# When the weight sums of a seven-product pair are made: with the pair's first piece instead of five pieces ahead

## Chip, cores and metric

The kernel runs on one core of a Trainium2 chip. The metric is the device time of one execution in microseconds (us); the time given for a kernel is the median of its runs. The tensor engine is called PE (its weight loads PEld), the vector engine DVE, the scalar engine ACT, GpSimd POOL, and the queue that issues the weight loads from memory SP.

## The reference, cut to what matters

Two decoder layers over 256 tokens of width 2048. Each layer is a token mixer followed by a gated feed-forward network with a causal convolution; all of it is products with large float32 weights.

```python
h = h + gla_mixer(...)      # ends in   o @ w_out      (2048 x 2048: "go" in the kernel)
h = h + conv_ffn(...)       # rms_norm(h) @ w_up, conv, silu(a)*u, @ w_down ("dn0")
k_blk, v_blk, k_mean = shared_kv(h, ...)
h = h + moba_mixer(...)     # ends in   o @ w_out      (2048 x 2048: "mo")
h = h + conv_ffn(...)       # "dn1"
```

The change touches the two output projections of the mixers, `go` and `mo`, and nothing else by its text.

## The kernel before

**Weights as a stream.** All weights pass through one `WeightStream`. A chunk is 128 x 2048 float32 (1 MB), loaded by SP (L96) into one of three buffers `wraw`. PE multiplies in a format of fewer bits, so each piece of up to 1024 columns of a chunk is split in two: ACT casts the high part (`whi`, L140), DVE subtracts it from the source and so makes the low part (`wlo`, L141). PE then does three products for each: high by high, low activation by high weight, high activation by low weight. A chunk's buffer is free for the next load when its last piece has been split. Most split pieces lie in three buffers each (`parts`); some pieces of the projections lie in a larger pool instead (`slot`).

**Pairs and seven products.** The output and down projections (`down`, L690 on) work through eight (or 22) pairs of 256 input rows, in two blocks of 1024 output columns. A block's order of pairs is written out in `ORDERS`; for the second block of `go` and for both of `mo` it is `0 2 1+ 3+ 4 | 5 6 7`. A plain pair needs two pieces of 1024 columns. A pair with a `+` takes seven products of quarters instead of eight, and needs sums of its weight quarters: its pieces are `b11` (the first 512 columns), `wide` (the second 1024), `t13` and `t24` (1024 each, sums). `_sums` makes `t13` and `t24` on DVE: L106 over 1024 columns, L107 and L108 over 512 columns each.

**When a piece is asked for.** `prefetch(i)` runs ahead of the product step `i`: the split of piece `n` is written down when `n` is within `AHEAD` (2) steps, plus 1 for pieces of projections, plus 2 for those in `deep`, which are the pieces of `go` and `mo`. Before the split of piece `n`, it looks through the next few pieces and, where one of them opens a seven-product pair, makes sure of that chunk's load and writes down its sums. In `go` and `mo` it looked at five pieces from `n` on.

**What sets the order.** The program is written down in one sequence; the framework's scheduler, with a timeline of its own, then sets each engine's order and the places of the buffers. Each engine works strictly through its own order, so an instruction that waits holds up what stands behind it.

**Ends of a block.** Products accumulate in PSUM (`acc`, three buffers of two banks, and two single banks `p`). At the last seven-product pair of a block ACT and DVE read the sums out into four tiles `c` (L756 to L760), POOL adds the residual to them by DMA (L762, from `x_tok` in `go`). Then come the tail pairs: first for the left half of the columns (products 2 and 4), then for the right (3 and 8), and after each half DVE adds the accumulator into `c` (L771). Products 2 and 3 share one accumulator `acc`, so the first right-half product of the tail waits until L771 has read the left half. PE transposes the finished columns (L795) while the next block runs; ACT (L253) and DVE (L255) make the next layer's operand `xw` from them, and the up-projection (L290, L293) follows.

Of the kernel before, what the change touches and what calls it, by code (L numbers as in the profile page):

```python
# [57 lines left out]
class WeightStream:  # L58
# [59 lines left out]
    def prefetch(self, i):  # L118
        nc = self.nc
        while self.n_split < len(self.halves):  # L120
            n = self.n_split
            c, o, kind = self.halves[n]
            if n > i + self.AHEAD + (kind != "plain") + 2 * (n in self.deep):
                break
            self._dma(c + 1)
            for c_, _, kind_ in self.halves[n:n + (5 if n in self.deep else 3)]:
                if kind_ == "b11" and c_ not in self.sums:
                    self._dma(c_ + 1)
                    self._sums(c_)
            src = self.sums[c][kind] if kind in ("t13", "t24") else self.tiles[c][:, o:o + 1024]  # L130
            if kind == "b11":
                src = src[:, :512]
            if kind != "plain" and n % 4 == 3 or n in self.deep and n % 2:
                hi, lo = self.slot([128, 1024], F32R, "whi"), self.slot([128, 1024], F32R, "wlo")
            else:
                hi = self.parts.tile([128, 1024], F32R, name="whi")
                lo = self.parts.tile([128, 1024], F32R, name="wlo")
            for a, b in ((0, 512), (512, 1024)) if n < 2 else ((0, src.shape[1]),):
                with self.tc.issue_after(self.first) if n + a else nullcontext():
                    one = nc.scalar.copy(hi[:, a:b], src[:, a:b])  # L140
                two = nc.vector.tensor_sub(lo[:, a:b], src[:, a:b], hi[:, a:b].bitcast(F32))  # L141
            self.latest = [one.ins, two.ins]
            self.split[n] = (hi, lo)
            self.n_split += 1
            if kind == "t24":
                del self.sums[c]
            if kind == "wide" and o == 1024 or kind == "plain" and (
                    self.n_split == len(self.halves) or self.halves[self.n_split][0] != c):
                del self.tiles[c]
                self._dma(c + 4)  # L150
# [969 lines left out]
```

## Time and profile before

| | |
|---|---|
| median of 3 runs | 2187.78 us (2187.05 to 2189.07) |
| profiled execution | 2188.65 us, its span from first to last instruction 2186.9 us |
| PE busy | 2169.1 us, 99% of the span |
| DVE busy | 1598.8 us, 73% |
| ACT busy | 1285.1 us, 59% |
| granted TensorE clock, mean | 0.999 |
| `go` on PE | 292 to 384 us of the span |
| `mo` on PE | from before 1385 to 1470 us |

Times in the rows are us from the span's start. A timeline row is: start, duration, engine, line, operation, tiles (out<-in), shape, count, and in brackets the idle time before it with what ended it. A row of the chain of waits is: start, duration, engine, tile and line. A row of the stretches is: the stretch, its length, then per engine busy us with the number of instructions, the granted clock, the share of the DMA engines that were busy, and GB/s. One product of 128 x 512 is shown with 0.39 us but the next begins 0.227 us after it, since products are pipelined.

### The profile page before, as it was taken

To read this page: it belongs to the slowest core of one execution; us is meant where nothing else is said; L and a number is where in the kernel's file an instruction comes from. 1 tells how busy PE (TensorE), PEld (TensorE's weight loads), DVE (VectorE), ACT (ScalarE), POOL (GpSimd) and SP (SyncE) were. 2 spreads that over 40 slices of the span, in tenths; PEclk is the share of its full clock that TensorE was granted. 3 is DMA by queue.
4 is the path that set the end of the run, shared out by engine and by line. 5 is a ranking of instruction groups with operands and counts; after the bars stand their busy time and mean duration, and the time that the engine had idled before them with its cause. 6 is when DMAs were issued, how large, how long until landed. Compare 5 with 4: busy or idle time off the path is not lost.

```text
span 2186.9 us, 26959 instructions
## 1 busy us (share of the span) xinstructions
PE 2169.1 (99%) x9693; PEld 1793.5 (82%) x9693; DVE 1598.8 (73%) x2202; ACT 1285.1 (59%) x1858; POOL 301.5 (14%) x448
## 2 busy tenths in 40 slices
PE   9999999999999999999999999999999999999999
PEld 7888887888888888887888888888888888887887
DVE  6655587667776767978967787776777676769887
ACT  6555765556555556555556676555656565655554
POOL 1011111111111111010013242011111111110000
PEclk9999999999999999999999999999999999999999
DMA  8465577577777777575677787676677777785655
GB/s 315 179 231 209 184 243 257 203 249 234 249 236 245 241 240 240 203 248 195 232 248 264 276 272 233 203 238 229 233 248 237 246 239 247 235 242 201 229 202 173
DMA packets 92248, 510.11 MB, mean 233 GB/s; under 512 B 13729, under 2 KB 14769, under 8 KB 42194
## 3 DMA queue, kind: packets, MB, share of 16 engines
q1 hardware_dynamic: 60722, 417.53, 54.1%
q0 software_dynamic: 30816, 90.28, 15.3%
q8 instruction: 76, 1.25, 0.2%
q10 hardware_dynamic: 576, 0.58, 0.1%
q14 instruction: 58, 0.48, 0.1%
HBM read 463.22 MB, written 45.11 MB: 232 GB/s over the span
## 4 chain that ended last, share of the span: by engine, by line
PE 91%; DMA 4%; DVE 3%; issue 1%; ACT 1%; SPq 0%; DVEq 0%; ACTq 0%
PE acc L290 44%; PE acc L293 22%; PE acc L730 13%; PE p L730 9%; DMA wraw<-w_dn 2%; DVE wlo L141 1%; DMA wraw<-w_go 1%; ACT whi L140 1%; DMA w2s<-w2a 0%; PE sT L561 0%; PE o L578 0%; DMA wraw<-w_v 0%; DVE t L106 0%; PE acc L795 0%; PE s L912 0%
## 5 line engine op out<-in xcount | busy, mean ns | idle before, releaser
L141 DVE TENSOR_TENSOR wlo<-wraw,whi 128x1024 fp32r<-128x1024 f32 (+1 forms) x786 | 929.9, 1190 | 446.4 <-ACT whi L140 425.5
L140 ACT CAST whi<-wraw 128x1024 fp32r<-128x1024 f32 (+1 forms) x786 | 799.6, 1027 | 675.4 <-PE acc L290 444.2
L290 PE MATMUL acc<-whi,xw 128*128 128x512 f32 x3840 | 952.2, 390 | 2.7 <-ACT whi L140 2.3
L290 PEld LDWEIGHTS acc<-whi,xw 128*128 128x128 f32 x3840 | 719.7, 188 | 154.1 <-ACT whi L140 3.1
L293 PE MATMUL acc<-wlo,xw 128*128 128x512 f32 x1920 | 514.1, 389 | 0.0
L293 PEld LDWEIGHTS acc<-wlo,xw 128*128 128x128 f32 x1920 | 360.2, 188 | 74.8
L730 PE MATMUL p<-whi,hid 128*128 128x512 f32 x572 | 204.1, 390 | 0.0
L730 PE MATMUL acc<-whi,hid 128*128 128x512 f32 x506 | 169.4, 389 | 0.0
L140 ACT CAST whi<-t 128x1024 fp32r<-128x1024 f32 x82 | 85.4, 1051 | 87.5 <-DVE t L108 25.3
L667 POOL DMA_DIRECT2D upT<-turned x176 | 114.1, 655 | 144.8 <-DMA turned<-z 55.9
L290 PE MATMUL acc<-whi,xkv 128*128 128x512 f32 x512 | 128.8, 391 | 0.0
L661 POOL DMA_DIRECT2D turned<-z x44 | 34.1, 775 | 680.1 <-DVE z L657 617.5
L730 PEld LDWEIGHTS p<-whi,hid 128*128 128x128 f32 x572 | 107.4, 188 | 22.2
L730 PE MATMUL acc<-whi,comb 128*128 128x512 f32 x328 | 107.7, 394 | 4.6 <-ACT whi L140 4.5
L730 PEld LDWEIGHTS acc<-whi,hid 128*128 128x128 f32 x506 | 95.0, 188 | 19.7
L290 PEld LDWEIGHTS acc<-whi,xkv 128*128 128x128 f32 x512 | 94.6, 188 | 18.6
L730 PE MATMUL p<-wlo,hid 128*128 128x512 f32 x286 | 106.3, 390 | 2.6 <-DVE wlo L141 2.6
L141 DVE TENSOR_TENSOR wlo<-t,whi 128x1024 fp32r<-128x1024 f32 x82 | 98.6, 1218 | 7.6 <-ACT whi L140 5.3
L676 ACT ACTIVATE au<-upT,cs 128x256 f32<-128x256 f32 x176 | 96.0, 595 | 10.8 <-DMA upT<-turned 10.7
L730 PE MATMUL acc<-wlo,hid 128*128 128x512 f32 x253 | 92.3, 390 | 0.8 <-DVE wlo L141 0.8
L762 POOL DMA_DIRECT2D c<-rows x24 | 21.2, 1073 | 463.2 <-DVE c L757 451.7
L682 DVE SCALAR_TENSOR_TENSOR au<-upT,cs,au 128x254 f32<-128x254 f32 x176 | 80.1, 477 | 0.0
(251 smaller groups left out, 1952.8 us busy)
## 6 DMA issues: line engine op xcount, KB each, us to landing
wraw<-w_up SPq DMA_DIRECT2D x176, 1024.0 KB, 4.9
wraw<-w_dn SPq DMA_DIRECT2D x88, 1024.0 KB, 4.8
turned<-z POOLq DMA_DIRECT2D x44, 512.0 KB, 3.5
upT<-turned POOLq DMA_DIRECT2D x176, 128.0 KB, 4.7
wraw<-w_g SPq DMA_DIRECT2D x16, 1024.0 KB, 4.8
wraw<-w_go SPq DMA_DIRECT2D x16, 1024.0 KB, 6.3
wraw<-w_mq SPq DMA_DIRECT2D x16, 1024.0 KB, 5.8
wraw<-w_kk SPq DMA_DIRECT2D x16, 1024.0 KB, 6.0
```

The source lines that it names most:

```text
L140: one = nc.scalar.copy(hi[:, a:b], src[:, a:b])
L141: two = nc.vector.tensor_sub(lo[:, a:b], src[:, a:b], hi[:, a:b].bitcast(F32))
L290: T.matmul(ps[:, t, :], xs(kt)[:, x0 + 128 * t:x0 + 128 * t + 128], hi[:, c:c + 512], start=kt == 0 and x0 == 0, stop=False)
L293: T.matmul(ps[:, t, :], xs(kt)[:, 128 * t:128 * t + 128], lo[:, c:c + 512], start=False, stop=kt == KT - 1)
L661: nc.gpsimd.dma_start(turned[J].rearrange("(a i) r q c -> (i r) a (q c)", a=4), z.rearrange("p (a q) t c -> p a (q t c)", a=4))
L667: nc.gpsimd.dma_start(f[32 * q:32 * q + 32].rearrange("p a (i c) -> p (a i) c", i=4), turned[J][:, :, q, :].rearrange("a r c -> r a c"))
L676: A.activation(au[:, i, :], t[:, i, :], AF.Identity, bias=col(cb + n), scale=col(cw + 2 * 2 * FT + n))
L682: V.scalar_tensor_tensor(au[:, i, 2:], t[:, i, :S - 2], col(cw + n), au[:, i, 2:], op0=OP.mult, op1=OP.add)
L730: T.matmul(p[n], x[xi], w[wi][:, 512 * f:512 * f + 512], start=n not in begun, stop=left[n] == 0)
L762: nc.gpsimd.dma_start(r[n], res(n // 2, 2 * b + n % 2), accum_op=OP.add)
```

## The change

For the pieces of `go` and `mo`, `prefetch` looks at one piece instead of five: the sums of a seven-product pair are written down when its own first piece (`b11`) is split, two pieces ahead of the first use of `t13`, and no longer up to four pieces earlier.

```diff
-            for c_, _, kind_ in self.halves[n:n + (5 if n in self.deep else 3)]:
+            for c_, _, kind_ in self.halves[n:n + (1 if n in self.deep else 3)]:
                 if kind_ == "b11" and c_ not in self.sums:
                     self._dma(c_ + 1)
                     self._sums(c_)
```

The instructions are the same in number and kind. What the diff doesn't tell is that the scheduler sets other orders, and other buffers, around them. Three places matter below. Numbers behind names tell buffers apart; in the second block of `go` the chunk of pair 0 is `wraw_2567`, of pair 2 `wraw_2608`, of pair 1+ `wraw_2648`, and of pair 3+ `wraw_2687` before and `wraw_2682` now.

ACT, at the start of the second block of `go`, before (a `whi` from `wraw` of 512 columns is a `b11`, one from `t13` a sum):

```order
L140 CAST whi_2644<-wraw_2548 128x1024
L140 CAST whi_2709<-wraw_2608 128x1024
L317 ACTIVATE junk_2703,ss_n_2419<-c0_2585 128x512
L317 ACTIVATE junk_2707,ss_n_2419<-c2_2587 128x512
L140 CAST whi_2767<-wraw_2648 128x512
L140 CAST whi_2683<-wraw_2567 128x1024
```

and further on in the same order:

```order
L253 ACTIVATE xw_2748<-acc_2743,cs_85 128x256
L140 CAST whi_2844<-wraw_2687 128x512
L253 ACTIVATE xw_2757<-acc_2743,cs_85 128x256
L140 CAST whi_2870<-t13_2762 128x1024
L140 CAST whi_2783<-wraw_2648 128x1024
```

The same two stretches of ACT now:

```order
L140 CAST whi_2644<-wraw_2548 128x1024
L140 CAST whi_2678<-wraw_2567 128x1024
L140 CAST whi_2720<-wraw_2608 128x1024
L140 CAST whi_2704<-wraw_2608 128x1024
L317 ACTIVATE junk_2698,ss_n_2414<-c0_2585 128x512
```

```order
L140 CAST whi_2807<-t13_2757 128x1024
L140 CAST whi_2778<-wraw_2648 128x1024
L140 CAST whi_2844<-wraw_2682 128x512
L253 ACTIVATE xw_2752<-acc_2738,cs_85 128x256
L140 CAST whi_2823<-t24_2758 128x1024
L140 CAST whi_2870<-t13_2839 128x1024
```

The second half of pair 0's chunk has moved ahead of pair 2 and of the `b11` of pair 1+, and the `wide` piece of pair 1+ (`whi_2783`, now `whi_2778`) no longer stands behind the `b11` and `t13` of pair 3+.

DVE, at the turn from the first to the second block of `go`, before:

```order
L141 TENSOR_TENSOR wlo_2645<-wraw_2548,whi_2644 128x1024
L771 TENSOR_TENSOR c0_2585<-c0_2585,acc_2420 128x512
L771 TENSOR_TENSOR c2_2587<-c2_2587,p4_2421 128x512
L141 TENSOR_TENSOR wlo_2710<-wraw_2608,whi_2709 128x1024
L771 TENSOR_TENSOR c3_2588<-c3_2588,p8_2422 128x512
L106 TENSOR_TENSOR t13_2662<-wraw_2648 128x1024
L141 TENSOR_TENSOR wlo_2768<-wraw_2648,whi_2767 128x512
```

and now:

```order
L141 TENSOR_TENSOR wlo_2645<-wraw_2548,whi_2644 128x1024
L141 TENSOR_TENSOR wlo_2679<-wraw_2567,whi_2678 128x1024
L141 TENSOR_TENSOR wlo_2721<-wraw_2608,whi_2720 128x1024
L771 TENSOR_TENSOR c0_2585<-c0_2585,acc_2415 128x512
L771 TENSOR_TENSOR c2_2587<-c2_2587,p4_2416 128x512
L141 TENSOR_TENSOR wlo_2705<-wraw_2608,whi_2704 128x1024
```

The first read of the accumulator (L771 into `c0`) has moved behind the low parts of pair 0's second half and of pair 2's first half; the sums L106 have left this place.

PE, at the end of `go`, where the up-projection begins (`whi_3070`), before, with the engines that an instruction waits for:

```order
L730 MATMUL acc_2797<-wlo_2990,go_2625 128x512 x2
L290 MATMUL acc_3137<-whi_3070,xw_2748 128x512 [waits DVE_49,PE_49]
L290 MATMUL acc_3137<-whi_3070,xw_2748 128x512 x7
L293 MATMUL acc_3137<-wlo_3071,xw_2748 128x512 x4
L290 MATMUL acc_3137<-whi_3105,xw_2757 128x512 [waits Activation_49]
L290 MATMUL acc_3137<-whi_3105,xw_2757 128x512 x7
L293 MATMUL acc_3137<-wlo_3106,xw_2757 128x512 x4
L290 MATMUL acc_3137<-whi_3123,xw_3012 128x512 [waits Activation_49]
L795 MATMUL hf_3150<-mk_86,c1_2943 128x2x2x32 [waits DVE_49]
```

and now:

```order
L730 MATMUL acc_2792<-wlo_2990,go_2625 128x512 x2
L290 MATMUL acc_3137<-whi_3070,xw_2743 128x512 [waits DVE_49,Activation_49]
L290 MATMUL acc_3137<-whi_3070,xw_2743 128x512 x7
L293 MATMUL acc_3137<-wlo_3071,xw_2743 128x512 x4
L795 MATMUL hf_3150<-mk_86,c1_2943 128x2x2x32
```

The transposes of `c1` (written by the last L771 of the block) no longer wait for DVE, since the first product of the up-projection, which stands ahead of them, has waited for that L771 already: its accumulator is now the one that this L771 reads. `mo` has the same difference at its end.

## Rows read from the trace of the kernel before

**Rows 1.** Page, part 1: busy us, share, instructions of each engine.
```profile
PE 2169.1 (99%) x9693; PEld 1793.5 (82%) x9693; DVE 1598.8 (73%) x2202; ACT 1285.1 (59%) x1858; POOL 301.5 (14%) x448
```
**Rows 2.** Timeline of PE, second block of `go`.
```profile
346.45 0.62 PE L730 MATMUL p<-wlo,go 128*128 128x512 f32 x2
350.58 0.79 PE L730 MATMUL acc<-whi,comb 128*128 128x512 f32 x1 [3.51 <-ACT whi L140]
...
355.92 0.84 PE L730 MATMUL acc<-whi,comb 128*128 128x512 f32 x3
```
**Rows 3.** Stretch behind that wait: busy us by engine, clock, DMA share, GB/s.
```profile
350.58:354.10 3.52, 3.52 (x9) 2.80 (x10) 3.52 (x5) 3.52 (x5) 0.00 (x0) 0.52 0.21 28
```
**Rows 4.** Chain of waits, 323 to 376 us.
```profile
323.28 8.27 DMA wraw<-w_go
331.65 1.06 ACT whi L140
...
337.49 1.15 DVE wlo L141
338.65 7.27 DMA wraw<-w_go
...
347.37 1.14 DVE t L106
348.54 2.00 ACT whi L140 x2
...
375.17 2.04 PE p L730 x9
```
**Rows 5.** Timeline of DVE, turn of the blocks of `go`.
```profile
316.52 1.22 DVE L141 TENSOR_TENSOR wlo<-wraw,whi 128x1024 fp32r<-128x1024 f32 x1 [1.06 <-ACT whi L140]
317.66 0.68 DVE L757 TENSOR_TENSOR c<-c,acc 128x512 f32<-128x512 f32 x1
...
329.33 0.69 DVE L771 TENSOR_TENSOR c<-c,acc 128x512 f32<-128x512 f32 x1 [3.19 <-PE acc L730]
...
332.73 1.23 DVE L141 TENSOR_TENSOR wlo<-wraw,whi 128x1024 fp32r<-128x1024 f32 x1 [2.11 <-ACT whi L140]
```
**Rows 6.** Timeline of PE: first right-half product of the tail of block one.
```profile
330.27 1.08 PE L730 MATMUL acc<-whi,go 128*128 128x512 f32 x4
```
**Rows 7.** Loads of `w_go`, all 16: time from issue to landing.
```profile
DMA to landing us min/median/max: 4.7/6.3/8.3
```
**Rows 8.** Stretches while the residual is added by DMA, and just after.
```profile
320.00:327.00 7.00, 7.00 (x32) 5.78 (x32) 6.14 (x7) 4.62 (x7) 2.65 (x3) 1.00 0.77 120
327.00:332.00 5.00, 5.00 (x24) 4.13 (x23) 1.28 (x2) 0.35 (x1) 1.14 (x2) 1.00 1.03 375
```
**Rows 9.** Timeline of DVE: one part of `xw`, one half sum.
```profile
348.42 0.48 DVE L255 SCALAR_TENSOR_TENSOR xw<-acc,cs,xw 128x256 fp32r<-128x256 f32 x1
348.82 0.68 DVE L107 TENSOR_TENSOR t<-t,wraw 128x512 f32<-128x512 f32 x1
```
**Rows 10.** Timelines of PE and DVE where the up-projections begin.
```profile
384.37 2.00 PE L290 MATMUL acc<-whi,xw 128*128 128x512 f32 x8
384.95 0.68 DVE L771 TENSOR_TENSOR c<-c,acc 128x512 f32<-128x512 f32 x1
1470.17 2.00 PE L290 MATMUL acc<-whi,xw 128*128 128x512 f32 x8
1470.74 0.68 DVE L771 TENSOR_TENSOR c<-c,acc 128x512 f32<-128x512 f32 x1
```
**Rows 11.** Timelines of DVE and PE, turn of the blocks of `mo`.
```profile
1417.37 0.69 DVE L771 TENSOR_TENSOR c<-c,acc 128x512 f32<-128x512 f32 x1 [2.52 <-PE acc L730]
1420.38 1.23 DVE L106 TENSOR_TENSOR t<-wraw 128x1024 f32<-128x1024 f32 x1 [2.32 <-DMA wraw<-w_mo]
1421.52 1.22 DVE L141 TENSOR_TENSOR wlo<-wraw,whi 128x1024 fp32r<-128x1024 f32 x1
1421.48 1.07 PE L730 MATMUL acc<-whi,ox 128*128 128x512 f32 x4
```
**Rows 12.** Stretches with the longest PE waits outside `go`: start of the kernel, `mo`.
```profile
11.40:13.50 2.10, 0.15 (x1) 0.00 (x0) 0.56 (x2) 1.09 (x2) 0.00 (x0) 1.00 1.04 423
13.50:17.00 3.50, 3.48 (x15) 2.85 (x16) 2.89 (x4) 1.89 (x4) 0.00 (x0) 1.00 1.02 406
1390.00:1400.00 10.00, 9.40 (x49) 7.36 (x48) 8.77 (x12) 7.53 (x12) 0.00 (x0) 1.00 0.28 107
```

## The prediction

> **What bounds the kernel now.** I read the busy shares first, then the timeline of the tensor engine for its gaps, then the chain of waits behind each gap. The tensor engine is busy 99% of the span [rows 1], so only a place where it stands still, or runs at the lower clock, can give anything back; DVE and ACT matter where a product waits for them. In the two stages that the change touches there is one such place of size: in the second block of `go` PE ends a run of products that begins at 346.45 and starts the next at 350.58, after 3.51 us idle that an ACT cast ended [rows 2]. Behind it the granted clock is 0.52, half of the full 2.4 GHz, for 3.5 us [rows 3]. The whole loss: from the product at 346.45 to that at 355.92 are 9.47 us [rows 2] with 18 products in them. Nine undisturbed ones take 2.04 us [rows 4], 0.227 each, so 18 take 4.08. **The place costs 5.4 us**, some 3.7 of waiting and 1.7 of low clock.
>
> Who made PE wait is in the chain [rows 4]: a load issued at 338.65 lands 7.27 us later; then comes a sum (L106, to 348.51), then two ACT casts from 348.54 to 350.54, then the product. By the order before, the load is the chunk of pair 3+, and the two casts are the `t13` of pair 3+ and, behind it, the `wide` piece of pair 1+. PE needs the second. It could have been cast long before, but stood in ACT's order behind two pieces of a later pair. And that pair's load was issued late because its buffer came free only with the DVE subtraction at 337.49, the second half of pair 0, which stood behind the sums and the `b11` of pair 1+.
>
> In `mo` the PE loss between 1390 and 1400 is 0.6 us of idle [rows 12]; it is where the attention values are still being made, and the change moves nothing there that PE waits for. I leave it.
>
> **The change, part by part.** No instruction is added or removed, and the order of SP's loads is the same. All gain or cost lies in PE's waits.
>
> *The old wait.* Now ACT casts the second half of pair 0 right after its predecessors, so the buffer is free, and the load of pair 3+ issued, about 11 us earlier; and the `wide` piece of pair 1+ stands ahead of everything of pair 3+. Both causes of the wait are gone: **-5.4 us**. It can't give more, since nothing else there holds PE; if one cause stayed, some of it would.
>
> *The turn of the blocks of `go`.* Before, DVE read the left half of the accumulator (L771) at 329.33, as soon as PE had finished it, and was done at 330.02 [rows 5]; PE went on with the right half at 330.27 [rows 6] without a wait. Now this L771 stands behind the low part of pair 2's first half. That one needs the load that the chain shows at 323.28 with 8.27 us to its landing at 331.55, then an ACT cast [rows 4]; before, it ran at 332.73 [rows 5], where nobody waited for it. What is queued behind it now is L771, and PE behind that. Price: landing 331.55, hand-over and cast 1.15, subtraction 1.14, L771 0.69, hand-overs 0.1: 334.6 against 330.27, 4.3 us. Part of that moves: before, DVE began the read-out L757 behind a subtraction that had waited 1.06 us for a late load [rows 5]. With the sums gone from ACT and DVE that load comes earlier; the residual's DMAs, and the load behind them, follow about 1.0 us sooner. So **+3.3 us**. The bounds come from the landing time. The loads of `w_go` take 4.7 to 8.3 us, median 6.3 [rows 7]. Issued at 322.3, a median landing gives 328.6 + 3.05 = 331.65, a wait of 1.4; the shortest gives none. I take the long one because the reason for it stays: from 320 to 327 the DMA engines are 0.77 busy but move 120 GB/s, the residual's slow transfers, and only then 375 GB/s [rows 8]; this load is issued into them again. Ends: 0 and 4.3.
>
> Here the clock is a second cost. The 3.5 us wait before was followed by the half clock [rows 3]; a wait of 2.1 us at the kernel's start was not: the stretch after it has 1.00 [rows 12]. A wait of 3.3 lies between, nearer to the one that cost 1.7. The Trainium skill (TensorE: Matmul & The Clock Gate, HAM oscillation — how this bites in real kernels) says that waits for a load between groups of products throttle the array, so that each next group starts cold; by that rule the turn costs 3.3 + 1.7 and the sum below is 1.7 higher, by the row of the shorter wait it is as it stands. I count it as a rival.
>
> *The sums of pair 3+.* They are now made after those of pair 1+ and after its low parts, shortly before use. From the four transposes that end ahead of pair 1+, PE's new order has 38 products to the first that reads the `t13` of pair 3+: 38 x 0.227 = 8.6 us. In that time: one ACT part of `xw` (0.5), on DVE two parts of `xw` (0.40 from one start to the next), two half sums (0.6 to 0.7), a `b11` (0.6), three low parts (1.14 each) and L106 (1.2) [rows 4, 9], 7.3 together, then the cast (1.06) and hand-overs (0.3): 9.2. **+0.6 us**; ends 0 and 2.2, the last being one sum and one cast in full view.
>
> *The first product of the up-projection*, after `go` and after `mo`. Its accumulator is now the one that the block's last L771 reads. In the trace before, that product started at 384.37 while L771 ran from 384.95 to 385.63; had it waited, it would have started at 385.68, 1.3 us later. In `mo`: 1470.17 against 1471.42, 1.3 again [rows 10]. DVE's order there still has one subtraction ahead of L771. **+1.3 us twice**; ends 0.9 each (the L771 and its hand-overs alone, which can't be hidden as PE's own last product feeds it) and 1.8.
>
> *The turn of the blocks of `mo`* has the same new order as that of `go`. There L771 ended at 1418.06 and PE needed it at 1421.48, 3.4 us of slack; the low part that is now ahead of it ran at 1421.52, but behind an L106 that had waited 2.32 us for another load and is no longer ahead [rows 11]. Unmoved it would make PE wait 2.0 us, moved up by the 2.3 nothing: **+0.2**, ends 0 and 2.0.
>
> Sum: -5.4 + 3.3 + 0.6 + 1.3 + 1.3 + 0.2 = **+1.3 us** on the span of 2186.9. The profiled execution took 2188.65, its span and 1.75 around it; the median of the runs is 2187.78. I add the difference to the median: **2189.1 us**.
>
> **Rivals.** *The clock falls at the new wait* (slower). Place: the turn of the blocks of `go`. Price: 3.3 us of wait and then 1.7 of half clock, as behind the old wait: +3.0, 2190.8; with the full 4.3 it is +4.0, and with a second such wait in `mo` up to +5. It decides from a PE idle time somewhere between 2.1 and 3.5 us. For it: the new wait is close to the old one. Against: it is a little shorter, and when the clock falls need not be the same in every run.
>
> *The load of pair 2 lands sooner* (faster). At the median landing the turn costs 1.4: -0.6, 2187.2; at the shortest it costs nothing: -2.0, 2185.8. For it: the load is issued a little earlier against the residual's DMAs, and the other loads of `go` mostly land sooner. Against: those DMAs move up with it.
>
> *The change doesn't do what it says*: pair 3+ still lands late and the old wait stays beside the new ones: +6.7, 2194.5. For it: the same three load buffers. Against: the casts that free the buffer stand ahead now.
>
> *None of the new waits is seen*: -5.4, 2182.4. For it: nothing but that PE was never stopped at these places before. Against: three of them follow from the order and from times in the trace.
>
> **How the numbers follow.** A measurement of this kernel can tell about 0.2% from no change, 4.4 us: below 2183.4 is faster, above 2192.2 slower. The forecast 0.43 (its own range 2187.5 to 2190.3); clock falls 0.30, of which 0.05 above 2192.2; sooner landing 0.17; old wait stays 0.05; no new wait 0.05. So faster 0.05, within 0.85, slower 0.10. The range goes from 2185.5, below the end of the sooner landing, to 2192.3, the clock rival with its bounds; it leaves out the last two cases and that rival's tail.
>
> **What would show it.** In the profile after, PE runs through 340 to 360 us without a wait. Around 330 it waits about 3.3 us for a DVE L771 that stands behind a low part released by an ACT cast that a `w_go` load released. The stretch behind it shows the clock at 1.00 or near 0.5, which settles the first rival. A wait of 1.3 us stands before the first L290 of both up-projections. The prediction is wrong if the wait around 330 is under 1 us or over 5, if an ACT cast still stops PE near 350, or if time is lost outside `go` and `mo`, where the order is the same.

## The result and the profile after

The changed kernel takes 2202.5 us (median of six runs, 2197.0 to 2204.7) against 2189.3 for the kernel before on the same chip (six runs too, 2187.1 to 2196.0): **a ratio of 1.0053, 95% interval 1.004 to 1.0065, half a per cent slower**. The profiled execution took 2202.19 us, its span is 2200.4: 13.5 us more than the span of before. Predicted was +1.3.

PE has the same instructions as before [rows 1] and is busy 6 us longer, in part because more of them run at half clock:

```profile
PE 2175.3 (99%) x9693; PEld 1795.7 (82%) x9693; DVE 1598.8 (73%) x2202; ACT 1282.4 (58%) x1858; POOL 301.8 (14%) x448
```

The list of PE's waits over the whole span (columns: who waited for whom, us in total, how often, longest) has three lines that end in DVE's L771, the add that reads a finished accumulator into the residual's tile. The list of before has no such line.

```profile
PE acc L795 <- DVE c L771: 3.9, 2, 2.3
...
PE acc L730 <- DVE c L771: 3.1, 1, 3.1
PE acc L290 <- DVE c L771: 2.6, 1, 2.6
```

Where the 13.5 us arise is read by comparing the start of the same product in both traces. The first right-half product at the turn of `go` goes from 330.27 [rows 6] to 333.81, +3.5. Past the place of the old wait PE is level again (+0.2 near 381). The first product of the up-projection goes from 384.37 [rows 10] to 389.54, and behind the half clock there PE is 6.9 late. The first down-projection adds 1.2. The turn of `mo` adds 4.0, after 0.3 gained ahead of it, and the first product behind `mo` goes from 1470.17 [rows 10] to 1482.92, 12.75 late. So, read where the lag is steady and rounded one by one: **up to the old wait +0.2, end of `go` +6.7, first down-projection +1.2, `mo` up to its turn -0.3, turn of `mo` +4.0, end of `mo` +1.1, the rest +0.7.**

*The turn of `go`* went as forecast but for the clock: DVE's timeline shows the low part that waited for ACT's cast, L771 behind it, and PE's timeline the wait for L771.

```profile
331.94 1.23 DVE L141 TENSOR_TENSOR wlo<-wraw,whi 128x1024 fp32r<-128x1024 f32 x1 [5.43 <-ACT whi L140]
333.08 0.68 DVE L771 TENSOR_TENSOR c<-c,acc 128x512 f32<-128x512 f32 x1
```
```profile
333.81 1.20 PE L730 MATMUL acc<-whi,go 128*128 128x512 f32 x4 [3.07 <-DVE c L771]
```

The clock then fell to half for a part of the stretch. The stretch behind that wait (columns: window, length, PE busy and products, granted clock, DMA share, GB/s), and those behind the two other large waits:

```profile
334.00:339.00 5.00, 5.00 (x16) 0.66 0.89 265
...
389.00:393.00 4.00, 3.46 (x9) 0.60 0.26 99
...
1435.00:1438.00 3.00, 3.00 (x10) 0.55 0.51 191
```

*The end of `go`* is where the forecast missed most. DVE's L771 there waits for no product: it waits for the residual's DMA, 5.59 us for one tile and 1.67 for the next, and a low part and half an `xw` stand between that one and the last L771. PE waits at the transposes of line 795 and again at the first L290.

```profile
384.23 0.69 DVE L771 TENSOR_TENSOR c<-c,p 128x512 f32<-128x512 f32 x1 [5.59 <-DMA c<-x_tok]
386.58 0.69 DVE L771 TENSOR_TENSOR c<-c,p 128x512 f32<-128x512 f32 x1 [1.67 <-DMA c<-x_tok]
387.19 1.22 DVE L141 TENSOR_TENSOR wlo<-wraw,whi 128x1024 fp32r<-128x1024 f32 x1
388.32 0.48 DVE L255 SCALAR_TENSOR_TENSOR xw<-acc,cs,xw 128x256 fp32r<-128x256 f32 x1
388.72 0.68 DVE L771 TENSOR_TENSOR c<-c,acc 128x512 f32<-128x512 f32 x1
```
```profile
384.97 0.55 PE L795 MATMUL acc<-mk,c 128*128 128x128 f32 x3 [1.55 <-DVE c L771]
...
389.54 2.66 PE L290 MATMUL acc<-whi,xw 128*128 128x512 f32 x6 [2.63 <-DVE c L771]
```

*The turn of `mo`* is the same thing, with 5.98 and 2.55 us of waiting in DVE; it is the first of the two that PE waits for:

```profile
1433.88 0.69 DVE L771 TENSOR_TENSOR c<-c,p 128x512 f32<-128x512 f32 x1 [5.98 <-DMA c<-rows]
1437.12 0.69 DVE L771 TENSOR_TENSOR c<-c,p 128x512 f32<-128x512 f32 x1 [2.55 <-DMA c<-rows]
```
```profile
1434.63 0.90 PE L795 MATMUL acc<-mk,c 128*128 128x128 f32 x3 [2.34 <-DVE c L771]
```

The kernel before was already near this. There the same L771 of `go` and of `mo` start at

```profile
377.18 0.69 DVE L771 TENSOR_TENSOR c<-c,p 128x512 f32<-128x512 f32 x1
...
1422.88 0.69 DVE L771 TENSOR_TENSOR c<-c,p 128x512 f32<-128x512 f32 x1
```

and the trace has their tiles' residual landing at 377.16 and 1422.85: each had waited some 0.15 us for it. So a landing that is later, against DVE's own order, holds DVE up at once; the prediction did not look at it.

Why is the residual late? The view of line 762, which issues it, second block of `go`, of before and then of after: the four transfers were issued 4.8 us (the first) to 2.0 us (the last) later, and the longest took 14.4 us instead of 8.3.

```profile
L762 POOL DMA_DIRECT2D c<-x_tok x4: 880/912/1287, 364.5 to 370.1; - x4
...
DMA to landing us min/median/max: 6.6/7.3/8.3
```
```profile
L762 POOL DMA_DIRECT2D c<-x_tok x4: 882/914/1291, 369.3 to 372.1; - x4
...
DMA to landing us min/median/max: 8.2/11.2/14.4
```

The DMA view of the second half of these transfers says what they met. Of before (372.0 to 378.5), and of after (378 to 385); columns: queue, packets, MB, share of 16 engines; q0 carries POOL's transfers, q1 the weight loads.

```profile
q0 software_dynamic: 508, 1.04, 80.8%
q1 hardware_dynamic: 72, 0.46, 23.9%
```
```profile
q1 hardware_dynamic: 256, 1.97, 69.4%
q0 software_dynamic: 255, 0.47, 36.1%
```

Before, the residual had the engines nearly alone, since no load was issued between 367.9 and 377.1. After, two loads of `w_up` go out at 374.2 and 377.5, and both queues send the same number of packets, 36 per us: the residual's carry 2 KB, the weights' 8 KB, so it gets a fifth of the bytes. The Trainium skill (DMA: Bandwidth & Descriptors, Queues, rings and completion order) says that a DMA engine takes turns between the queues it has work for, a whole packet from one before it switches, and by its count a packet is typically a group of some 9 to 17 descriptors. 256 against 255 of the profile's packets agree with turns of equal size; how large a turn is, these rows do not show.

The first four loads of `w_up` in SP's timeline, of before and of after:

```profile
361.41 15.98 SPq L96 DMA_DIRECT2D wraw<-w_up  x4
```
```profile
365.77 12.07 SPq L96 DMA_DIRECT2D wraw<-w_up  x4
```

### The profile page after: what moved, and what is told of

It is laid out like the page before. It is cut to its first block, busy times and chain, and to the rows that moved or that the text cites. A ratio compares the mean times of both kernels' runs of the same rounds, so it can differ in the third digit from the quotient of the medians.

```text
span 2200.4 us, 26957 instructions
## 1 busy us (share of the span) xinstructions
PE 2175.3 (99%) x9693; PEld 1795.7 (82%) x9693; DVE 1598.8 (73%) x2202; ACT 1282.4 (58%) x1858; POOL 301.8 (14%) x448
## 3 DMA queue, kind: packets, MB, share of 16 engines
q0 software_dynamic: 30816, 90.28, 15.3%
q8 instruction: 76, 1.25, 0.2%
## 4 chain that ended last, share of the span: by engine, by line
PE 82%; issue 8%; DMA 5%; DVE 3%; POOL 1%; ACT 1%; SPq 0%; DVEq 0%; POOLq 0%; ACTq 0%
PE acc L290 42%; PE acc L293 21%; PE acc L730 10%; PE p L730 7%; DMA wraw<-w_dn 2%; DVE wlo L141 2%; DMA c<-x_tok 1%; DMA c<-rows 1%; DMA w2s<-w2a 0%; POOL turned L393 0%; DMA probs<-z 0%; PE sT L561 0%; PE o L578 0%; ACT whi L140 0%; DMA wraw<-w_v 0%
## 5 line engine op out<-in xcount | busy, mean ns | idle before, releaser
L290 PE MATMUL acc<-whi,xw 128*128 128x512 f32 x3840 | 954.2, 390 | 5.6 <-DVE c L771 2.6
L290 PEld LDWEIGHTS acc<-whi,xw 128*128 128x128 f32 x3840 | 720.7, 188 | 158.2 <-ACT xw L253 5.4
L730 PE MATMUL p<-whi,hid 128*128 128x512 f32 x572 | 204.1, 390 | 0.0
L730 PE MATMUL acc<-whi,hid 128*128 128x512 f32 x506 | 169.4, 389 | 0.0
L290 PE MATMUL acc<-whi,xkv 128*128 128x512 f32 x512 | 128.8, 391 | 0.0
L730 PEld LDWEIGHTS p<-whi,hid 128*128 128x128 f32 x572 | 107.4, 188 | 22.3
L730 PEld LDWEIGHTS acc<-whi,hid 128*128 128x128 f32 x506 | 95.0, 188 | 19.7
L290 PEld LDWEIGHTS acc<-whi,xkv 128*128 128x128 f32 x512 | 94.6, 188 | 18.6
L730 PE MATMUL p<-wlo,hid 128*128 128x512 f32 x286 | 106.5, 391 | 2.7 <-DVE wlo L141 2.6
L730 PE MATMUL acc<-whi,comb 128*128 128x512 f32 x328 | 106.5, 391 | 1.4 <-ACT whi L140 1.4
L676 ACT ACTIVATE au<-upT,cs 128x256 f32<-128x256 f32 x176 | 96.0, 595 | 14.5 <-DMA upT<-turned 14.5
L730 PE MATMUL acc<-wlo,hid 128*128 128x512 f32 x253 | 92.3, 390 | 0.8 <-DVE wlo L141 0.8
L680 DVE SCALAR_TENSOR_TENSOR au<-upT,cs,au 128x255 f32<-128x255 f32 x176 | 76.4, 471 | 5.7 <-ACT au L676 5.6
```

What stands on the lines that cost most here:

```text
L290: T.matmul(ps[:, t, :], xs(kt)[:, x0 + 128 * t:x0 + 128 * t + 128], hi[:, c:c + 512], start=kt == 0 and x0 == 0, stop=False)
L676: A.activation(au[:, i, :], t[:, i, :], AF.Identity, bias=col(cb + n), scale=col(cw + 2 * 2 * FT + n))
L680: V.scalar_tensor_tensor(au[:, i, 1:], t[:, i, :S - 1], col(cw + 2 * FT + n), au[:, i, 1:], op0=OP.mult, op1=OP.add)
L730: T.matmul(p[n], x[xi], w[wi][:, 512 * f:512 * f + 512], start=n not in begun, stop=left[n] == 0)
```

## The experiments

They ran on three other chips, each beside runs of the kernel before, whose medians there were 2194.5 to 2195.7; so ratios are compared. Theory A: the residual's transfers land late and L771 waits for them. Theory B: L771 is late by its place in DVE's order. Theory C: the transfers are late because they are issued later, not because of the loads beside them.

**One stage alone.**

```diff
-self.halves[n:n + (5 if n in self.deep else 3)]
+self.halves[n:n + (1 if n in self.near else 5 if n in self.deep else 3)]
```

> Look-ahead 1 in the first output projection (go) alone, 5 in the second (mo) as before. The changed kernel's profile lost 7.0 us against before by the first up-projection after go (PE ran 6.98 us behind at the same instruction), 1.0 more in the first down-projection and 5.0 in mo and right behind it. If the two projections lose apart, this gives before +7 to +8: 2194 to 2197 us, a ratio of 1.0032 to 1.0037, with mo's rows as in before. If the loss of mo is a follower of go's (a state carried on), go alone costs all 13.

Ratio 1.0016 (0.9999 to 1.0032): half of the loss that was expected, which only the upper end of the interval reaches.

> Look-ahead 1 in mo alone, 5 in go. If the two lose apart: before +4 to +5.5 us, a ratio of 1.0018 to 1.0025, and go keeps its wait of 3.7 us near 350 with the clock at half behind it. The 1.0 us that the changed kernel lost in the first down-projection, which has the same order in both, should then be absent; if it appears here too, it is not go's doing but the run's.

Ratio 1.002 (1.0005 to 1.0035). PE's waits in the trace of `go` alone, from 290 to 400 us (lines are two lower in this file), then in that of `mo` alone from 1400 to 1500:

```profile
PE acc L732 <- DVE c L773: 2.9, 1, 2.9
PE acc L797 <- DVE c L773: 2.1, 1, 2.1
PE acc L292 <- DVE c L773: 1.3, 1, 1.3
```
```profile
PE acc L797 <- DVE c L773: 3.8, 1, 3.8
PE acc L292 <- DVE c L773: 1.0, 1, 1.0
```

Each stage makes its own waits; nothing is carried from `go` to `mo`. So it is with the residual: the longest transfer of `go`'s second block takes 14.5 us with `go` alone and 8.5 with `mo` alone, that at the turn of `mo` 9.2 and 15.3. The sum, 0.36%, is less than the 0.53% of both, but the intervals cover that.

**The residual left out**, with the small look-ahead and with the old one.

```diff
-for n in (0, 2, 1, 3):
-    nc.gpsimd.dma_start(r[n], res(n // 2, 2 * b + n % 2), accum_op=OP.add)
+if name.startswith("dn"):
+    for n in (0, 2, 1, 3):
+        nc.gpsimd.dma_start(r[n], res(n // 2, 2 * b + n % 2), accum_op=OP.add)
```

> The changed kernel (look-ahead 1) with the eight residual transfers of go and of mo left out (line 762, four of 256 KB in each block), so the residual is not added there; all else is as it was. Theory A (the residuals land late because 1 MB weight loads now run beside them; DVE's L771 waits for the landing, and PE for L771): the four waits of PE at 385, 389.5, 1434.6 and 1482.9 (1.6+2.6+2.3+0.9) and two of the three stretches at half clock (2 x 1.7) go, 10.8 us, and the wait at the turn of go (3.1+1.7) goes too if it was a load held up by the residual: 2186 to 2192 us. Theory B (L771 is late because more of DVE's row stands ahead of it, the residual only lands at the same time): the waits stay and the time is that of the changed kernel, 2200 to 2203.

Ratio 0.9974 (0.9959 to 0.999), span 2186.8. The orders of PE, ACT and SP are those of the changed kernel, and in DVE's only four L771 stand a place or two earlier. All its waits from 290 to 400 us:

```profile
PE acc L290 <- ACT xw L253: 0.9, 1, 0.9
PE acc L730 <- ACT whi L140: 0.4, 1, 0.4
```

The waits on L771 at the turn and the end of `go` and at the turn of `mo` are gone, and no half clock is left in either stage. **This convicts the residual's transfers**, also of the wait at the turn of `go`, whose load they held up: issued at nearly the same time (322.3 against 322.5), it lands at 327.0 instead of 330.8. DVE's order at that turn is the same in both, with L771 behind the low part, and PE does not wait. So theory B falls as the cause alone.

> The kernel before (look-ahead 5) with the same sixteen residual transfers left out. It is the base for the run above. Theory A: the old wait near 350 (3.7 + 1.7 of half clock) hung on a load held up by the residuals of go's first block, so it goes or shrinks: 2181 to 2185 us, and the small look-ahead costs 0 to 6 us against this base rather than 13. Theory B: 2187 as before, and the small look-ahead costs 13 us here too.

Ratio 0.9978 (0.9962 to 0.9994). As a ratio that is what was expected: 2181 to 2185 against 2187.8 is 0.997 to 0.999. The old wait near 350 is 2.1 us instead of 3.5, but not by the way of theory A: its load was issued at 339.2 and landed at 347.2, no sooner than before (338.7 and 345.9). PE, 1.3 us late from the kernel's start on, came to the place 2.6 us late, after a wait of 0.95 near 323 for the gated operand, and left it 1.25 us late. So the wait only became shorter because part of it was spent earlier. Where the 0.2% comes from these traces do not show. Beside the run above: without any residual the small look-ahead is worth nothing that can be measured in the time, though in that run's trace `go` is 3.2 us shorter than in the kernel before.

**Fewer, larger transfers**: two of 512 KB for four of 256 KB.

```diff
-nc.gpsimd.dma_start(r[n], res(n // 2, 2 * b + n % 2), accum_op=OP.add)
+for t in range(2):
+    nc.gpsimd.dma_start(two[t], res(t, 2 * b, 1024), accum_op=OP.add)
```

> The changed kernel (look-ahead 1); in go and mo the four residual transfers of a block are sent as two, each over 1024 columns instead of 512 (rows of 4 KB in memory instead of 2 KB), the same bytes. Theory A (the transfers lose time beside the weight loads, packet for packet: in the changed kernel's trace the two queues moved 35 and 36 packets per us between 378 and 385 us, 66 KB against 290): if a packet is now 4 KB, they land in about half the time, the waits of PE at 385, 389 and 1434 mostly go, and the time is before to before +5, ratio 1.000 to 1.0023. If the packets stay at 2 KB, nothing changes in the traffic and the ratio stays near 1.005. Theory C (what counts is that they are issued later, 2.0 us for the last one of go's second block): the two transfers wait for all adds, are issued no sooner, and the ratio stays near 1.005 even with larger packets.

Ratio 0.9995 (0.9981 to 1.001): the loss is gone. But not by the way expected. The last transfer still took 12.8 us (14.4 before the edit), not half: its packets have 4 KB now, but in the trace each takes 0.33 us, where one of 2 KB took 0.19. It was issued at 365.1 instead of 372.1, some 5 us of this because the wait and half clock at the turn of `go` were absent, the rest because two issues take less of POOL's time than four. DVE still waits:

```profile
DVE cc L779 <- DMA cc<-x_tok: 6.8, 2, 6.2
```

PE waits 1.4, 1.2 and 0.9 us at the end of `go` and keeps its clock. This edit moves some of PE's and DVE's order too, so it is no clean test between A and C.

> The kernel before (look-ahead 5) with the same two wide transfers per block. Theory A: the old wait near 350, which shrank from 3.7 to 2.3 without any residual, shrinks to between these, so 0 to 2 us under before, ratio 0.999 to 1.000. Theory C: no change.

Ratio 0.9997 (0.9984 to 1.001), no change, as theory C had it. The old wait was 3.8 us, not smaller; here A's number failed.

**Look-ahead 3.**

> Look-ahead 3, the value of the down-projections, for go and mo, residuals as they were. Its order differs from the changed kernel's in fewer places than from that of before. Theory A: what counts is when the weight loads stand; if those of the end of go and mo are issued as late as in the changed kernel (loads of w_up beside the residuals, landing 11 us after issue), it costs the same +10 to +13 us; if they are issued as in before, 0 to +3. Theory B (DVE's row): the sums stand two pieces earlier, so about half of the loss, +5 to +7, whatever the loads do.

Ratio 1.0013 (0.9998 to 1.0027). Issued 1 us earlier than in the changed kernel, the last residual transfer of `go` took 11.7 us and landed at 382.8; PE waits for an `xw` 1.6 us at the end of `go` instead of 1.55 and 2.63 for L771, with no half clock there. At the turn of `go` it still waits 3.45 us for L771, with half clock behind it, and at the turn of `mo` 1.5. The time lies between the two kernels, as the landing time does.

**The residual loaded ahead, added by POOL.**

```diff
-nc.gpsimd.dma_start(r[n], res(n // 2, 2 * b + n % 2), accum_op=OP.add)
+x_n = ahead[n // 2][:, 512 * (n % 2):512 * (n % 2) + 512]
+nc.gpsimd.tensor_tensor(r[n], r[n], x_n, op=OP.add)
```

> The changed kernel (look-ahead 1); the residual of a block of go and mo is loaded at the block's beginning into two tiles of its own and added by POOL (four adds of 128x512) where line 762 stood; nothing is left out. Theory A: no transfer lies between the adds and L771 any more, so the waits at 385, 389 and 1434 go with their half clock as they did without the residual, and the time is that of the run without residual, ratio 0.997 to 1.000, if POOL's adds take 1 to 2 us each. Theory B: waits stay, ratio 1.005. It would be worse than the changed kernel if POOL's adds were over 3 us each or the early loads delayed weight loads at the block's beginning.

Ratio 0.9993 (0.9981 to 1.0004). The waits at the ends and the turns are down to 0.9 us, or gone, and have no half clock behind them, but a load at the block's beginning now comes late: PE waits 3.4 us for an ACT cast at 316, with half clock behind it.

**More loads beside the residual**, in the kernel before.

```diff
+if b == 1 and not name.startswith("dn"):
+    for t in range(2):
+        extra = slot([128, 1024], F32, f"extra{t}")
+        nc.sync.dma_start(extra, w_up0[0, :131072].rearrange("(p c) -> p c", p=128))
```

> The kernel before (look-ahead 5) with 1 MB more of weight loads (two tiles of 512 KB that nothing reads) in the load queue, just ahead of the up-projection's first loads, in the second block of go and of mo, where the residual transfers run. Look-ahead and sums stay as they were. Theory A (the residuals are late because weight loads run beside them): they land later than the 8.3 and 9.1 us of before, by some 2 to 5 us, L771 waits for them, and PE stops at the end of go and of mo for 1 to 4 us, partly with half clock behind it: ratio 1.001 to 1.005. Theory C (it is the later issue): the issue times do not move, so the landings and the time stay, ratio 1.000.

Ratio 0.9999 (0.9986 to 1.0011). The residual did land later, 10.2 us after issue in `go` instead of 8.3, and 13.1 instead of 9.1 in `mo`. Its rows in `mo`, of the kernel before and then of this run:

```profile
L762 POOL DMA_DIRECT2D c<-rows x4: 884/924/1317, 1451.4 to 1456.9; - x4
...
DMA to landing us min/median/max: 7.2/7.6/9.1
```
```profile
L766 POOL DMA_DIRECT2D c<-rows x4: 884/926/1312, 1454.1 to 1456.9; - x4
...
DMA to landing us min/median/max: 8.9/11.5/13.1
```

The last transfer is issued at the same time and takes 4.0 us longer. The added loads themselves had landed by then (1452.2); they pushed the weight loads behind them into the residual's flight. DVE waits for it in `mo`, where before it waited 1.1 us:

```profile
DVE c L775 <- DMA c<-rows: 3.8, 2, 2.9
```

PE does not wait in either place. So loads beside the residual lengthen it, against C; and **in the order of before, DVE's longer wait costs PE nothing**, since PE does not need L771 soon. A's price is not settled by this: PE itself runs 1.8 us (`go`) and 2.7 us (`mo`) later here than in the kernel before, so against PE the last landing is late by 1.2 and 1.3 us only, where in the changed kernel's `go` it is 7.9.

**A better place for the early load**: go's two blocks load it between the gates' first and second product.

```diff
+if hd == 1:
+    early.update({("go", b): fetched("go", b, from_input) for b in range(2)})
```

> Look-ahead 1 with the residual loaded ahead and added by POOL, as in the run with the preload; but go's two blocks are loaded between the gates' first and second product, where the queues stood empty (near 250 us), not at the blocks' beginnings. The preload's profile had PE waiting 3.6 us at 316 with half the clock behind it, 1.4 at 329 and 1.1 at 337, where the load of a weight chunk landed 9.5 us after its issue. Theory A (every one of these is a load held up by another): they go, 3.6+1.7+1.4 = 6 to 7 us less than the preload, near the run without residual: ratio 0.9965 to 0.998. If they are due to POOL's adds or to the order, they stay, ratio 0.999.

Ratio 0.9985 (0.9972 to 0.9997). The wait at 316 fell from 3.4 to 0.6 us and its half clock is gone; waits of 1.2 and 1.1 near 322 and 326 for the gated operand remain, and 0.8 for L771 at the turn.

> The same early load with look-ahead 5. It shows what the look-ahead is worth when no residual transfer can be late. If the small look-ahead is then better (as the two runs without the residual had it, 2189.9 against 2192.1), this is 1 to 4 us slower than the run before it in this list: it keeps the old wait near 350, at 2.3 us or so with its half clock: ratio 0.998 to 1.000. If the order of large look-ahead is the better one in itself, it is the faster of the two, ratio 0.995 to 0.997.

**Ratio 0.998 (0.9972 to 0.9989), faster than both kernels**, 2190.7 against 2195.7: the old look-ahead of 5 with the residual loaded early. The old wait near 350 is down to 0.8 us, without half clock:

```profile
PE acc L745 <- DVE go L304: 1.3, 1, 1.3
PE acc L745 <- ACT go L303: 0.9, 1, 0.9
PE acc L745 <- ACT whi L140: 0.8, 1, 0.8
```

It shrank because PE comes to it 3.1 us later, after the two other waits, near 322 and 325; behind it PE is 0.5 us later than in the kernel before, and the half clock, 1.7 us, is what is saved there. That the residual caused the old wait is not shown. With the residual loaded early no difference between the look-aheads can be measured: the intervals of the two runs overlap.

**The changed kernel again.**

> The changed kernel again, unaltered, beside the others: ratio 1.004 to 1.0065 as first measured, and in the profile the waits at the turn of go, the ends of go and mo and the turn of mo. The 1.0 us lost in the first down-projection, where the order is the same, differs if it was chance. If the ratio is nearer to 1.003 here, part of the first one came from that chip.

Ratio 1.0059 (1.0045 to 1.0073), with the same waits in the same places (L730 2.5, L795 6.8 in two, L290 3.8 in two).

## Why the prediction failed, point by point

- **Old wait, -5.4: right.** PE runs through 340 to 357 us, at clock 1.00.
- **Turn of `go`, +3.3: right in place, cause and size** (3.07, and the chain was the load, the cast, the low part, L771). **The clock was wrong:** it fell, 1.7 us, the first rival. That rival's bound, an idle time between 2.1 and 3.5 us, does not hold either: the wait in [rows 12] is 1.97 us (2.1 is the length of the stretch), and the clock fell after 2.34 and 1.90 in other places. Together the place costs what the old one had cost, and the gain is gone.
- **Sums of pair 3+, +0.6: right.** PE waits 0.43 near 357, within the ends.
- **First product of the up-projection, +1.3 each: the step that failed, behind `go`.** Measured 2.63 there, plus 1.55 at the transposes just ahead, plus 1.7 of half clock. Of the other 0.8 of the 6.7, 0.44 are four transposes that before stood at 377.05 and now stand here, and 0.3 belong to the two waits, which the profile counts from the modelled end of the product before, 0.16 us after the next could begin. The term let L771 run where it had run before and asked only what now hangs on it. It never asked when L771's *other* operand lands: the tile that the residual's DMA writes. Behind `mo` it was right within its ends: PE is idle for 0.87 and starts 1.0 later, released by L771 and by `xw` within 0.02 us of each other. Without the residual both waits are 0.87.
- **Turn of `mo`, +0.2: mis-sized for the same reason.** I asked for the load ahead of the first L771 and gave 3.4 us of slack, and that one did not stop PE. The next L771 did, whose tile's residual landed at 1433.9 instead of 1422.9, 3.2 us more than PE's own lag of 7.8: 2.34 of wait, 1.7 of clock.
- **"The order of SP's loads is the same"** was true and the wrong thing to look at. Their times moved, because each load waits for a buffer that DVE's splits free: in `go` the last two of `w_go` went out 5 and 6 us later, and the first four of `w_up` within 12 us instead of 16. I had used that row for the turn of `go` (the residual's slow transfers hold up a load, [rows 8]) and did not turn it round: loads hold up the residual.
- **Lost outside `go` and `mo`: 1.2 us** in the first down-projection, and 0.7 behind `mo`; the prediction had named such a loss as a sign against it. The profiles speak for scatter: against before, the first down-projection is longer by 0.2 us with look-ahead 3, by 0.3 and 1.3 without the residual (old and small look-ahead), by 0.8 in the second profile of the changed kernel, and by 2.6 with `mo` alone, where `go` is as before.

The rivals had no case for this: none let the residual land late. The range, to 2192.3, took the clock's cost once; it fell three times.

What stays open: how much of the loss is due to the later issue (2.0 us for the last transfer of `go`) and how much to the longer flight (6.1). No run held the new order with the old traffic. And there is no trace of the kernel before from the other three chips, so where the run with the early load gains its 0.2% is not shown either.

## What to carry to other kernels

When an order changes, go through *every* operand of the instructions on which somebody newly waits, those that a DMA writes above all, and lay the new issue times of loads beside the transfers in flight: an unchanged order of issue is not an unchanged time. A transfer that stands between a result and its user should not run beside a weight stream, and packets of twice the size did not make it short here; load such an operand early, in a quiet stretch, and add it on an idle engine. A wait that is removed by shifting a stream can come back where the stream now runs, as it did here. And look in the trace of before for instructions that start just as their DMA lands: they have no slack.

## What was not expected of the hardware

- POOL's accumulating transfers of 256 KB took from 4.2 us, first of their four, to 15.0 us beside weight loads, in the profiles of the two kernels.
- The clock does not follow the length of PE's wait alone. It fell after 1.55 and 2.63 close together, after 2.34, and after 3.07; in the run with `go` alone after 1.90 at the kernel's start, where 1.97 in the profile of before did not bring it down [rows 12]. In five of the experiments' profiles it fell behind two waits of 0.8 and 1.0 us near 1010 to 1020, which the kernel before has as well, without it. The windows of the run without the residual and of before:

```profile
1009.00:1013.00 4.00, 4.00 (x12) 0.57 0.39 107
```
```profile
1009.00:1013.00 4.00, 2.81 (x11) 1.00 0.68 278
```

- So it can differ from run to run: one of the changed kernel's six executions shows a mean clock of 1.000 and a span of 2195.2, and 2200.4 less three times 1.7 is 2195.3.
- An add of 128x512 on POOL took 1.3 to 2.4 us, where DVE takes 0.69.
